# Seven half-size products in the down-projection of one token block, with weight differences made beforehand on VectorE

## The chip, the cores and the metric

The kernel runs on one core of one Trainium2 chip. The metric is device time in microseconds of one execution; the median of three runs of the kernel before is 2796.26 us (2793.03 to 2800.73). The engines are TensorE (PE; its weight loads are listed apart as PEld), VectorE (DVE), ScalarE (ACT), GpSimd (POOL) and SyncE (SP), which here issues nearly all DMAs.

## The reference

One layer of a network with two kinds of attention and a feed-forward part, on 2048 prompt tokens and 128 sample tokens (8 sequences of 16), all in fp32. What matters here is the feed-forward part behind it:

```python
def conv_ffn(h, buf, w_up, w_conv, b_conv, w_down):
    u = h @ w_up                                   # [S, 1024] @ [1024, 5632]
    ext = jnp.concatenate([buf.astype(u.dtype), u], axis=1)
    y = b_conv
    for j in range(CONV_W):                        # 3
        y = y + ext[:, j:j + S] * w_conv[j]
    gate, up = jnp.split(y, 2, axis=-1)
    out = (jax.nn.gelu(gate, approximate=True) * up) @ w_down   # [S, 2816] @ [2816, 1024]
    return out, ext[:, S:]
```

The layer then adds `rms_norm(ffn, norm_g[3])` to its input rows and returns them.

## The kernel before, in words

**Precision.** A matmul works on values in a shorter format (fp32r). So each fp32 operand is split into a high part (a cast by ScalarE) and a low part (the operand less the high part, by VectorE); `split`, in the profile L1265 (cast) and L1266 (subtraction). `mm3` (L93) makes three matmuls of each product: high x high (L95), high x low (L96), low x high (L97). A weight or activation piece is loaded as fp32 by DMA into a raw buffer, split, and used.

**Blocks.** The 17 token tiles of 128 rows are worked on in three blocks (FBLOCKS): tiles 0 to 5, 6 to 11, and 12 to 15 with the sample tile. For each block there is an up stage and a down stage.

**Up stage.** 22 column groups f of 128 gate and 128 up columns. The product is already made as seven products of half-size blocks in Winograd's form of Strassen's method (P1 to P7; `product`, L1411); the differences of the weights are made on VectorE in the first block (L1282) and kept in DRAM (`wsd`) for the others. Behind it come the convolution, GELU and the product of gate and up, giving a row buffer `gt` (128 columns x 768 tokens), which is stored to DRAM as `gd` (L1519). While the last groups run, the first tiles of `gd` are fetched back (`fetch`, L1454) and split (`split_g`, L1465).

**Down stage.** For each half `dh` of the 1024 output columns: six accumulators in PSUM, one per token tile, 512 columns each; for each of the 22 k (128 rows of w_down) 6 tiles x 3 matmuls of 128 x 512, the tile of g being the stationary and the weights the moving operand. `load_down` (L1311) loads and splits the weights in chunks of four k, one chunk ahead, into buffers `wh` and `wl` (two each). Tiles of g go through `w3` buffers, four of them, so two pairs of high and low. At the end of a half `evacuate` (L1334) copies the accumulators (VectorE, L1340) and sums the squares (ScalarE, L1344); the halves go to DRAM (f0d, f1d). In the same stage `ahead.step()` is called once per k: it advances `h2_units` (L1057 and on: loading, scaling and transposing the rows of the next block, and making its seven activation operands B) and `later` (L1369): scaling the finished rows of the block before (VectorE, L1376), adding the input (GpSimd, L1377) and storing (GpSimd, L1378).

**Buffers.** Raw pieces of 512 columns come from `quad` (tag "q", 11 buffers), rows of 1024 from `row` (tag "yq", 4 buffers). Loads wait for a free buffer.

**Order.** The program is written in the order of the loops; a planner built into the framework then reorders each engine's instructions by an estimated timeline. Each engine, and SP's queue of DMA issues, runs in order: an instruction that waits holds back all behind it. `tc.keep_in_program_order` fixes the order of some DMAs against each other.

## Time and profile before

| | |
|---|---|
| median of three runs | 2796.26 us (2793.03 to 2800.73) |
| the profiled execution's span, first to last instruction | 2784.7 us |
| busy: PE / DVE / ACT / POOL | 2723.8 / 1876.3 / 1409.1 / 437.4 us |
| up stages of the three blocks, roughly | 1313 to 1641, 1836 to 2154, 2349 to 2616 us |
| down stages, roughly | 1641 to 1836, 2155 to 2349, 2618 to 2777 us |

The profile is of one execution, and its times are microseconds from its first instruction. Nothing is listed of that execution's own time around the span; the median of the runs is 11.6 us above it. A row of groups reads: line, engine, operation, output <- inputs (buffer numbers left out), shapes, count | busy time, mean duration of one in ns | idle time of the engine just before them, and what ended it. Durations of successive operations on one engine overlap a little, so busy time is less than count times mean. A row of windows gives the stretch, its length, then busy us (and instructions) of each engine, the granted TensorE clock, the DMA share and GB/s.

### The profile page before, as it was taken

The numbers are of one execution on the slowest core, as the hardware profiler recorded it, in microseconds if no ns is written. First come the engines' busy times: TensorE is split into PE (matmuls) and PEld (weight loads), VectorE is DVE, ScalarE is ACT, GpSimd is POOL, SyncE is SP. The second block draws the span as 40 slices with busy tenths as digits, with TensorE's granted clock in tenths as the row PEclk, the third lists the DMA queues.
The fourth block names the chain that finished last, engine by engine and source line by source line (L and its number), as shares of the span: only waits on it lengthen the run. The fifth ranks groups of instructions, "written<-read, shape, count | busy, mean of one in ns | idle before, by whom it ended". The sixth has DMA issues, their size and how long they took to land.

```text
span 2784.7 us, 47088 instructions
## 1 busy us (share of the span) xinstructions
PE 2723.8 (98%) x16587; PEld 2548.3 (92%) x16587; DVE 1876.3 (67%) x3447; ACT 1409.1 (51%) x2836; POOL 437.4 (16%) x895
## 2 busy tenths in 40 slices
PE   8999999999999999999999999999999999999998
PEld 7899999998899998888999988899999878999887
DVE  5344455656556668666999986457877864888855
ACT  4355555644356666544454555345455543555543
POOL 1000010212000003244111110011111310222220
PEclk9999999999999999999999999999999999999999
DMA  5544355557555555356655455644544774555585
GB/s 185 155 119 136 103 174 162 164 157 217 162 173 148 144 179 171 107 176 227 187 172 167 167 176 174 219 142 153 160 152 141 276 263 152 172 179 180 192 309 190
DMA packets 311883, 486.05 MB, mean 175 GB/s; under 512 B 55426, under 2 KB 150622, under 8 KB 311518
## 3 DMA queue, kind: packets, MB, share of 16 engines
q1 hardware_dynamic: 271134, 442.92, 50.1%
q10 hardware_dynamic: 38592, 33.83, 3.6%
q0 software_dynamic: 1920, 6.29, 0.6%
q8 instruction: 130, 2.13, 0.3%
q14 instruction: 107, 0.88, 0.1%
HBM read 359.36 MB, written 126.70 MB: 175 GB/s over the span
## 4 chain that ended last, share of the span: by engine, by line
PE 55%; DVE 2%; DMA 1%; issue 1%; ACT 1%; POOL 1%; SPq 0%; DVEq 0%; POOLq 0%; ACTq 0%
PE uec L95 6%; PE uec L96 6%; PE uec L97 6%; PE dn L97 4%; PE dn L96 4%; PE dn L95 4%; PE ua L97 3%; PE ua L95 3%; PE ua L96 3%; PE dnm L97 2%; PE dnm L95 2%; PE dnm L96 2%; PE wo L97 2%; PE wo L95 2%; PE wo L96 2%; PE ub L96 1%
## 5 line engine op out<-in xcount | busy, mean ns | idle before, releaser
L95 PE MATMUL uec<-B,wuh 128*128 128x384 f32 (+1 forms) x720 | 234.9, 328 | 2.2 <-DVE uu L1419 1.1
L96 PE MATMUL uec<-B,wuh 128*128 128x384 f32 (+1 forms) x720 | 235.1, 327 | 0.0
L97 PE MATMUL uec<-B,wul 128*128 128x384 f32 (+1 forms) x720 | 233.9, 327 | 0.0
L1266 DVE TENSOR_TENSOR gl<-gr,gh 128x768 fp32r<-128x768 f32 (+3 forms) x141 | 120.4, 863 | 145.8 <-ACT gh L1265 144.5
L1265 ACT CAST gh<-gr 128x768 fp32r<-128x768 f32 (+3 forms) x141 | 102.0, 735 | 200.1 <-PE dn L96 183.2
L1265 ACT CAST wuh<-wu 128x512 fp32r<-128x512 f32 x255 | 141.7, 617 | 112.1 <-PE uec L96 103.2
L95 PE MATMUL dn<-wdh,gh 128*128 128x512 f32 x466 | 182.4, 391 | 2.3 <-DVE ug L1419 2.3
L96 PE MATMUL dn<-wdl,gh 128*128 128x512 f32 x466 | 183.4, 394 | 0.0
L97 PE MATMUL dn<-wdh,gl 128*128 128x512 f32 x466 | 167.9, 396 | 0.0
L1266 DVE TENSOR_TENSOR wul<-wu,wuh 128x512 fp32r<-128x512 f32 x255 | 164.6, 683 | 2.8 <-DMA x2d<-mx 2.8
L393 DVE CUSTOM_DVE_ANT_0 tmp<-s,nb 128x640 f32<-128x640 f32 (+4 forms) x128 | 94.4, 737 | 96.6 <-PE s L383 94.8
L95 PE MATMUL vo<-wi_h,hT 128*128 128x256 f32 x544 | 155.1, 285 | 0.6 <-DVE mt L199 0.6
L97 PE MATMUL vo<-wi_h,hT 128*128 128x256 f32 x544 | 155.6, 286 | 0.0
L96 PE MATMUL vo<-wi_l,hT 128*128 128x256 f32 x544 | 154.8, 285 | 0.0
L95 PEld LDWEIGHTS uec<-B,wuh 128*128 128x128 f32 x720 | 135.0, 188 | 4.2 <-DVE uu L1419 1.6
L95 PE MATMUL qk<-hT,wi_h 128*128 128x384 f32 (+1 forms) x384 | 128.7, 335 | 7.4 <-ACT qk_st L224 6.6
L96 PEld LDWEIGHTS uec<-B,wuh 128*128 128x128 f32 x720 | 135.2, 188 | 0.2
L97 PEld LDWEIGHTS uec<-B,wul 128*128 128x128 f32 x720 | 135.1, 188 | 0.0
L406 DVE TENSOR_TENSOR ptl<-pt,pth 128x640 fp32r<-128x640 f32 (+4 forms) x128 | 93.6, 737 | 57.1 <-ACT pth L405 56.0
L394 ACT ACTIVATE tmp<-tmp,mn 128x640 f32<-128x640 f32 (+4 forms) x128 | 97.6, 762 | 64.6 <-DVE mn L393 61.9
L96 PE MATMUL qb<-hT,wi_h 128*128 128x384 f32 (+1 forms) x384 | 127.8, 333 | 0.0
L96 PE MATMUL qk<-hT,wi_h 128*128 128x384 f32 (+1 forms) x384 | 127.6, 332 | 0.0
(412 smaller groups left out, 8873.0 us busy)
## 6 DMA issues: line engine op xcount, KB each, us to landing
wu<-in_w_up SPq DMA_DIRECT2D x220, 256.0 KB, 4.1
wu<-wsd SPq DMA_DIRECT2D x176, 256.0 KB, 4.2
wdr<-in_w_down SPq DMA_DIRECT2D x132, 256.0 KB, 5.6
gr<-gd SPq DMA_DIRECT2D x78, 384.0 KB, 3.6
wi_raw<-in_w_in SPq DMA_DIRECT2D x52, 512.0 KB, 4.0
wsd<-ws SPq DMA_DIRECT2D x88, 256.0 KB, 2.8
gd<-g SPq DMA_DIRECT2D x44, 384.0 KB, 3.5
kraw<-kTd SPq DMA_DIRECT2D x112, 128.0 KB, 3.2
```

The source lines that it names most:

```text
L95: nc.tensor.matmul(out, ah, bh, start=start, stop=False, skip_group_check=onto)
L96: nc.tensor.matmul(out, ah, bl, start=False, stop=False, skip_group_check=onto)
L97: nc.tensor.matmul(out, al, bh, start=False, stop=stop, skip_group_check=onto)
L393: nc.vector.tensor_tensor_reduce(o_, s_, b_, 1.0, 3e38, ALU.add, ALU.min, accum_out=mn)
L394: nc.scalar.activation(tmp[:, :n], tmp[:, :n], AF.Exp, bias=mn, scale=-1.0, accum_out=rsum[:, i % 4, hh:hh + 1])
L406: nc.vector.tensor_tensor(s.ptl[:, sl, qc], ptv, s.pth[:, sl, qc], op=ALU.subtract)
L1265: nc.scalar.copy(h, r)
L1266: nc.vector.tensor_tensor(l, r, h, op=ALU.subtract)
```

## The change: what it does

In the second block (FAST = (1,)) the down-projection is computed with the same scheme of seven products. G is cut into A11, A12, A21, A22 (token tiles 0 to 2 or 3 to 5; the first or the last 11 of the 22 k), w_down into B11, B12, B22, B21 in the same way (11 k each, 512 columns each). The weight operands T1 to T4 are differences of the four B blocks.

- `folds` loads w_down in 22 pieces of [128, 4, 256] into `row` buffers, makes four differences on VectorE and stores them in DRAM (`wtd`). One half of a piece's work is done in two of three k of the first block's down stage, and in three of four column groups of the second block's up stage.
- The second block's up stage runs through the columns in the order 0, 11, 1, 12, ... . `store_a` stores A11, A12, A22 and the four sums and differences S1 to S4, which are made in place in the `gt` buffers of the two columns (four VectorE operations of 384 columns); the buffer of column f is held until that of f + 11 is there. A21 alone isn't needed.
- The second block's down stage is a sequence of seven products of 11 k x 3 tiles. Three of the six accumulators make a set; products 0, 2, 4 and 6 add up in set 0, products 1, 3 and 5 are in set 1. `leave` takes a set out while the other is used (ScalarE copies after products 0, 2, 4, 6; VectorE additions after 1, 3, 5). `ahead.step()` is called once every two k.
- Weights are loaded in chunks of four k as before (`down_rows`); a chunk now serves 36 matmuls, not 72. A tile of A holds two k of 384 tokens (`fetch_a`, `split_a`).
- w_down is laid out in DRAM in the four blocks; the other blocks' loads have the same sizes.
- `quad` has 12 buffers, `row` 6, `drs` 2; the scratch memory for GpSimd's DMAs is 4096 bytes.

```diff
+NK = NF // 2
+FAST = (1,)
+ORDERS = [[f for k in range(NK) for f in (k, k + NK)] if b in FAST else list(range(NF)) for b in range(3)]
...
-        return ffn.p3.tile([P, 512], F32, tag="q", name=name, bufs=11)
+        return ffn.p3.tile([P, 512], F32, tag="q", name=name, bufs=12)
...
-        return ffn.p3.tile([P, D], F32, tag="yq", name=name, bufs=4)
+        return ffn.p3.tile([P, D], F32, tag="yq", name=name, bufs=6)
...
+    def folds():
+        v4 = lambda t: t.rearrange("p (a n) -> p a n", a=4)
+        def load(k, c):
+            t = v4(row(f"fold{k}_{c}"))
+            tc.keep_in_program_order(nc.sync.dma_start(t, v4(I["w_down"][k])[:, :, c * 256:(c + 1) * 256]))
+            return t
+        def combine(t):
+            a, b, c, d = [t[:, i] for i in range(4)]
+            for o, x, y in ((a, b, a), (b, c, b), (c, c, a), (d, d, c)):
+                nc.vector.tensor_tensor(o, x, y, op=ALU.subtract)
+        for k in range(NK):
+            for c in range(2):
+                t = load(k, c)
+                yield
+                combine(t)
+                tc.keep_in_program_order(nc.sync.dma_start(v4(wtd[k])[:, :, c * 256:(c + 1) * 256], t))
+                yield
...
+    SEQUENCE = [("A11", B11, 0, False), ("A12", B21, 1, False), ("S2", T2, 0, True), ("S4", B22, 1, False),
+                ("S3", T3, 0, True), ("S1", T1, 1, False), ("A22", T4, 0, True)]
...
+        def store_a(f, gt):
+            put = lambda what, k, src: nc.sync.dma_start(ad[b, what][:, k, :], src)
+            first, second = gt[:, 0:384], gt[:, 384:768]
+            if f < NK:
+                put("A11", f, first)
+                held[f] = gt
+                return
+            k = f - NK
+            put("A12", k, first)
+            put("A22", k, second)
+            gt1 = held.pop(k)
+            a11, a21, a12, a22 = gt1[:, 0:384], gt1[:, 384:768], first, second
+            nc.vector.tensor_tensor(a11, a11, a21, op=ALU.subtract)
+            nc.vector.tensor_tensor(a21, a21, a22, op=ALU.add)
+            nc.vector.tensor_tensor(a22, a22, a11, op=ALU.subtract)
+            nc.vector.tensor_tensor(a12, a12, a22, op=ALU.subtract)
+            for what, src in (("S3", a11), ("S1", a21), ("S2", a22), ("S4", a12)):
+                put(what, k, src)
...
-        for f in range(NF):
+        for fi, f in enumerate(ORDERS[b]):
...
-            nc.sync.dma_start(gd[b][f][:, :nt * P], gt[:, :nt * P])
+            if fast:
+                store_a(f, gt)
+                if fi % 4 < 3:
+                    next(fold, None)
+            else:
+                nc.sync.dma_start(gd[b][f][:, :nt * P], gt[:, :nt * P])
...
+            for p, (_, _, set_, onto) in enumerate(SEQUENCE):
+                for c in range(3):
+                    wh, wl = pend
+                    if c < 2:
+                        pend = load_product(b, p, c + 1)
+                    elif p < 6:
+                        pend = load_product(b, p + 1, 0)
...
+                    for k in range(4 * c, min(4 * c + 4, NK)):
+                        i = 6 * p + k // 2
+                        if k % 2 == 0:
+                            if i >= 1:
+                                split_a(i + 1)
+                                fetch_a(i + 4)
+                        wk = slice(k % 4 * 512, k % 4 * 512 + 512)
+                        ah, al = parts[i]
+                        for j in range(3):
+                            tt = slice(k % 2 * 384 + j * P, k % 2 * 384 + (j + 1) * P)
+                            mm3(sets[set_][j], ah[:, tt], al[:, tt], wh[:, wk], wl[:, wk],
+                                start=not onto and k == 0, stop=k == NK - 1, onto=onto)
+                        steps += 1
+                        if steps % 2 == 0:
+                            ahead.step()
+                leave(p)
...
+                    if b == 0 and (dh * NF + k) % 3 < 2:
+                        next(fold, None)
...
-    nc = bacc.Bacc("TRN2", target_bir_lowering=False, num_devices=1)
+    nc = bacc.Bacc("TRN2", target_bir_lowering=False, num_devices=1, dynamic_dma_scratch_size=4096)
```

154 lines of the change are left out of this document (127 added, 27 removed).

## The prediction

> **What bounds the kernel now.** I read the page's engine lines, its slices and its chain first, then the busy time by stage.
>
> ```profile
> span 2784.7 us, 47088 instructions
> ...
> PE 2723.8 (98%) x16587; PEld 2548.3 (92%) x16587; DVE 1876.3 (67%) x3447; ACT 1409.1 (51%) x2836; POOL 437.4 (16%) x895
> ...
> PE   8999999999999999999999999999999999999998
> ...
> PEclk9999999999999999999999999999999999999999
> ...
> PE 55%; DVE 2%; DMA 1%; issue 1%; ACT 1%; POOL 1%; SPq 0%; DVEq 0%; POOLq 0%; ACTq 0%
> ```
>
> TensorE is busy in every slice, at a granted clock of nine tenths or more, and it holds the chain: a matmul that goes is time that goes, as long as the engines that feed TensorE keep up. By stage (up of the first block, its down, up of the second, its down; columns: length, then busy time of PE, PEld, DVE, ACT, POOL, clock, DMA share, GB/s):
>
> ```profile
> 1313.00:1641.00 328.00, 322.00 (x1827) 318.55 (x1825) 302.79 (x457) 167.79 (x266) 61.74 (x87) 0.99 0.54 179
> 1655.00:1836.00 181.00, 180.42 (x805) 146.72 (x804) 101.61 (x140) 87.11 (x146) 5.02 (x17) 1.00 0.56 184
> 1840.00:2150.00 310.00, 310.00 (x1781) 310.00 (x1780) 239.98 (x357) 156.93 (x257) 41.49 (x92) 1.00 0.48 154
> 2166.00:2349.00 183.00, 182.60 (x812) 147.55 (x811) 115.07 (x151) 85.37 (x145) 35.07 (x41) 1.00 0.68 232
> ```
>
> The stage that the change rewrites is the last row: 183 us, TensorE without a gap, VectorE at 63%.
>
> **The change, part by part.**
>
> *Matmuls.* The second block's down stage has 22 k x 6 tiles x 2 halves x 3 = 792 matmuls of 512 columns; seven products of 11 k x 3 tiles x 3 make 693. The timeline of that stage gives the distance from one to the next:
>
> ```profile
> 2311.10 0.39 PE L95 MATMUL dn<-wdh,gh 128*128 128x512 f32 x1
> ...
> 2315.94 0.39 PE L95 MATMUL dnm<-wdh,gh 128*128 128x512 f32 x1
> ```
>
> Between these two starts lie 21 steps, 4.84 us, so 0.2305 us each. 99 x 0.2305 = 22.8 us go. The accumulators lie in two sets, and each is emptied while the other is filled for 99 x 0.2305 = 22.8 us, so I cost their emptying, and the step into the next block, at nothing; without that cover three copies of 0.68 us would stand on the path once a product.
>
> *VectorE and the feed of the seven products.* In steady state a tile of A (two k, 384 columns each) serves 18 matmuls as a tile of g did, so the splitting of A costs what that of g cost. But each weight piece now serves 9 matmuls, not 18: 77 pieces are split, not 44, and a chunk of four lasts 36 x 0.2305 = 8.3 us, not 16.6. The stage is not even: the preparation of the third block (h2_units) and the finished rows of the first (later) fill its first half, and they still take one step per 18 matmuls, so they fall on the first four products. The windows of before, its VectorE groups in 2166-2258, two of 2258-2349, one of GpSimd, and the DMA sum of 2166-2258:
>
> ```profile
> 2166.00:2258.00 92.00, 91.60 (x417) 73.35 (x416) 76.57 (x100) 51.07 (x88) 32.85 (x33) 1.00 0.79 273
> ...
> 2258.00:2304.00 46.00, 46.00 (x201) 37.43 (x201) 20.53 (x28) 19.73 (x36) 2.22 (x8) 1.00 0.77 267
> 2304.00:2349.00 45.00, 45.00 (x197) 36.77 (x196) 17.98 (x24) 14.56 (x23) 0.00 (x0) 1.00 0.38 114
> ```
>
> ```profile
> L1266 DVE TENSOR_TENSOR gl<-gr,gh 128x768 fp32r<-128x768 f32 x18 | 21.3, 1184 | 3.5 <-ACT gh L1265 3.4
> L1266 DVE TENSOR_TENSOR wdl<-wdr,wdh 128x512 fp32r<-128x512 f32 x22 | 16.4, 804 | 0.0
> L1376 DVE SCALAR_TENSOR_TENSOR f<-f,drs,norm_row 128x512 f32<-128x512 f32 x12 | 10.0, 831 | 4.5 <-DMA f<-f0d 4.5
> L1085 DVE SCALAR_TENSOR_TENSOR x2r<-x2r,n_rs,g 128x1024 f32<-128x1024 f32 x4 | 6.2, 1540 | 5.2 <-POOL n_rs L84 5.2
> ...
> L1340 DVE COPY fr<-dnm 128x512 f32<-128x512 f32 x2 | 1.3, 678 | 0.0
> ...
> L1106 DVE TENSOR_TENSOR B<-b,B 128x256 fp32r<-128x256 f32 x3 | 1.2, 412 | 0.0
> ```
>
> ```profile
> L1266 DVE TENSOR_TENSOR gl<-gr,gh 128x768 fp32r<-128x768 f32 x21 | 20.1, 958 | 47.1 <-ACT gh L1265 47.1
> L1266 DVE TENSOR_TENSOR wdl<-wdr,wdh 128x512 fp32r<-128x512 f32 x18 | 11.5, 685 | 3.8 <-ACT wdh L1265 3.8
> ```
>
> ```profile
> L1377 POOL TENSOR_TENSOR f<-f,x 128x512 f32<-128x512 f32 x12 | 22.0, 1834 | 35.7 <-DVE f L1376 26.2 <-DMA gr<-gd 9.5
> ```
>
> ```profile
> DMA packets 10786, 25.08 MB, mean 273 GB/s; under 512 B 1280, under 2 KB 1280, under 8 KB 10779
> ```
>
> VectorE worked 76.6 of 92 us. To that come 22 more weight subtractions (another 16.4 us), the accumulator additions in place of copies (6 x 0.68 - 1.3 = 2.8 us), and the last five differences of A that run over from the up stage (5 x 0.55 = 2.8 us): 98.6 us. TensorE needs for four products 396 x 0.2305 = 91.3 us and some 3 us of transposes, 94 us. So VectorE asks for 4 us more than there are, and its in-order waits come on top: 3.4 + 4.5 + 5.2 = 13.1 us in the rows above, of which a part vanishes when VectorE itself is late. The loss is between 0 (the pieces of the fifth product may come one chunk, 8.3 us, late, and the last products have room) and 98.6 + 13.1 - 94 = 18 us. I take 8, nearer to the busy sum than to the waits, since those rows show waits of an engine that had time. The last three products: 33 x 0.685 + 18 x 0.96 + 6 x 0.68 = 44 us of VectorE in 68: covered. ScalarE in the first four: 51.1 + 22 x 0.62 + six copies and three squares of some 0.6 = 70 of 94 us: covered. DMA: 25.1 MB + 22 x 0.26 MB + ten late stores of 0.2 MB = 33 MB in 94 us, 350 GB/s, against these (the first from the third block's down stage):
>
> ```profile
> 2650.00:2680.00 30.00, 30.00 (x131) 24.31 (x130) 18.82 (x25) 11.08 (x17) 13.98 (x15) 1.00 1.05 400
> 2189.00:2212.00 23.00, 23.00 (x109) 18.76 (x109) 20.70 (x26) 13.83 (x23) 10.20 (x11) 1.00 0.97 345
> ```
>
> 400 GB/s went by while TensorE ran without a gap, so it fits, but with nothing to spare; that keeps 18 us in the range.
>
> *Up stage of the second block.* Its order of columns (f, f + 11) costs nothing: the loads are the same. VectorE gets 44 operations of 384 columns and 28 of 256 (7 of the 22 weight pieces, four differences each):
>
> ```profile
> L1493 DVE TENSOR_TENSOR x<-x,uec 128x384 f32<-128x384 f32 x22 | 12.2, 553 | 11.3 <-PE uec L97 11.2
> ```
>
> 240.0 + 44 x 0.55 + 28 x 0.41 = 276 of 310 us, 89%. Two of the four differences overwrite a tile whose store must have landed, and block VectorE until then; the stores of the sums stand in SP's queue ahead of the next weight loads and wait for them. The page's rows for such a store and for a weight load:
>
> ```profile
> gd<-g SPq DMA_DIRECT2D x44, 384.0 KB, 3.5
> ...
> wdr<-in_w_down SPq DMA_DIRECT2D x132, 256.0 KB, 5.6
> ```
>
> The built order puts four other VectorE operations, some 2.7 us, between the product and the first overwrite, so about 1 us is left per pair, 11 us, and VectorE is occupied for 287 of 310 us, 93%. The first block's up stage stands at 302.8 of 328 us, 92%, and what it pays is seen in TensorE's waits of 1313-1641:
>
> ```profile
> PE ua L97 <- DVE wul L1266: 3.0, 2, 1.6
> PE uec L95 <- DVE uu L1419: 1.1, 1, 1.1
> PE uec L95 <- DVE ug L1419: 1.0, 1, 1.0
> ```
>
> Between 0 and 5; much of the 5 stands at that stage's beginning, so I take 2. 77 stores of 0.2 MB for 22 of 0.39 and 7 pieces of 1 MB moved add 14 MB, 45 GB/s to 154: hidden.
>
> *Down stage of the first block.* 15 of the 22 pieces: 60 differences x 0.41 = 24.7 us on VectorE, 126 of 181 us; 15 loads and 15 stores of 512 KB make 184 into 270 GB/s. Each store waits in SP's queue for VectorE, and behind it the weight loads. Covered by VectorE's 30% and by buffers; without that a store holds the queue some 2 us, 30 in all. Between 0 and 3, I take 1.
>
> *Buffers and the small DMA scratch.* 12 and 6 buffers for 11 and 4 change the planner's order from the first up stage on: between -4 and +4, taken 0 (that stage's waits above are about all there is to gain). GpSimd's 12 stores in the seven products are one per 7.8 us; a smaller ring could make one wait for the one before, 0 to 3 us, taken 0, since GpSimd is busy 33 of 92 us.
>
> Sum: -22.8 + 8 + 2 + 1 = -11.8 us. The profiled span of 2784.7 us becomes 2772.9. The median of the runs shown, 2796.26, is 11.6 above that span; I leave that as it is and get **2784.4 us**.
>
> **The rivals.** *All hidden.* If the first four products keep TensorE fed and the others cost 1, it is -21.8: 2774. For it: VectorE had 15 us idle in 92; against: it needs all of them.
>
> *GpSimd and VectorE exclude each other.* While GpSimd adds (22.0 us), the subtraction of g took 1184 ns against 958, that of weights 804 against 685: 18 x 0.226 + 22 x 0.119 = 6.7 us lost. With VectorE full there is no idle time in which the rest could hide: 22.0 - 6.7 = 15.3 us more, net +3.5, 2800. The Trainium skill, SBUF — State Buffer, section "Who interferes with whom", says that a VectorE instruction with two SBUF inputs and a GpSimd instruction that reads SBUF lock each other out for a whole instruction; by that rule this rival holds, and the rows above agree that there is a price but show under a third of it.
>
> *Slower: weights late.* Of twelve small buffers the preparation of the third block uses eight, so in the first products loads may not run ahead. Then a chunk's last piece comes after its landing, four casts and a subtraction:
>
> ```profile
> wdr<-in_w_down SPq DMA_DIRECT2D x18, 256.0 KB, 5.7
> ...
> x2r<-x2d SPq DMA_DIRECT2D x4, 512.0 KB, 7.2
> ```
>
> 5.7 + 4 x 0.62 + 0.69 = 8.9 us, against 8.3 for a chunk of four and 6.2 for one of three: 14 x 0.6 + 7 x 2.7 = 27 us late over the stage, which with the 3 us of the other stages gives +7 (2804); each further us of landing adds 21. From 5.8 us on it is slower beyond noise; at 6.5 it is 2821. For it: DMA near its highest rate and the row of 7.2. Against it: ScalarE hardly waited for weights before (4.7 us in the stage).
>
> ```profile
> ACT wdh L1265 <- DMA wdr<-in_w_down: 4.7, 5, 1.3
> ```
>
> *It saves nothing,* because the steps between matmuls lengthen by a seventh: +3, 2799. Nothing speaks for it; the shapes are the same.
>
> **How the numbers follow.** 0.3% of 2796 is 8.4 us, about what a measurement of this kernel can tell from no change. Forecast 0.42 (its own range 2776 to 2792; 0.34 below 2787.9, 0.08 above), all hidden 0.20, exclusion 0.12, weights late 0.22, no saving 0.04. Faster 0.54, same 0.08 + 0.12 + 0.04 = 0.24, slower 0.22. The range goes from 2771 (nothing lost, and the buffers gain 3) to 2806, where it leaves out most of the slower case and little else.
>
> **What would show it.** 99 fewer matmuls, the seven products ending some 14 us sooner after their start than 183 us; gaps of TensorE in the first four, ended by VectorE's subtractions, none in the last three; VectorE over 95% in the first four; 0 to 5 us of gaps in the second up stage. The prediction is wrong if those gaps exceed 20 us, if a DMA ends them, or if the unchanged stages move by more than 4 us.

## The result: slower by 0.4%, and the profile after

The changed kernel takes 2807.65 us (median of five runs, 2801.63 to 2811.27) against 2794.01 us for the kernel before on the same chip: 1.0040 times as long, 95% interval 1.0029 to 1.0051. That is outside the predicted range and on the other side of the kernel before. The profiled execution of the changed kernel is the fastest of its five, 6.0 us below the median, so the stages below account for that execution and not for the median. Its page begins with the span and the busy time by engine:

```profile
span 2799.9 us, 47375 instructions
...
PE 2717.2 (97%) x16488; PEld 2541.4 (91%) x16488; DVE 1940.9 (69%) x3610; ACT 1426.7 (51%) x2879; POOL 458.8 (16%) x895
```

The 99 matmuls are gone (16587 to 16488), yet the span grew, and TensorE's busy time fell by 6.6 us, not by 22.8. Slices of 70 us don't show why. So I cut each trace by what TensorE works on: an up stage runs from the first to the last start of its up matmuls, and the rest of the block, its down stage with the turn into the next, follows. The times are starts of matmuls in the trace, in us:

| kernel | ahead of the blocks | up 1 | down 1 | up 2 | down 2 | up 3 | down 3 | span |
|---|---|---|---|---|---|---|---|---|
| before, as profiled first | 1313.5 | 338.0 | 185.0 | 328.3 | 184.5 | 276.1 | 159.5 | 2784.7 |
| before, profiled again | 1316.0 | 335.4 | 185.1 | 328.3 | 185.3 | 276.1 | 164.9 | 2791.1 |
| **after** | 1318.4 | **341.9** | **197.7** | 331.3 | **170.5** | 277.9 | 162.2 | 2799.9 |

Three stages moved by much. The seven products (down 2) save 14.0 us. The first block's down stage, where the weight differences are made, loses 12.7. The first up stage, in which the change alters no instruction but has other buffer counts, loses 4 to 6.5. The rows of the windows for down 1, up 2 and down 2, first of the kernel after, then of the kernel before (columns as in the prediction):

```profile
1660.30:1858.00 197.70, 187.06 (x818) 150.48 (x817) 124.78 (x202) 91.18 (x151) 9.73 (x20) 0.98 0.75 247
1858.00:2189.30 331.30, 329.96 (x1879) 327.24 (x1878) 281.28 (x447) 168.54 (x280) 45.71 (x101) 1.00 0.62 195
2189.30:2359.80 170.50, 163.92 (x708) 131.43 (x707) 132.68 (x189) 103.86 (x188) 39.01 (x47) 0.97 0.81 282
```

```profile
1651.50:1836.50 185.00, 183.77 (x819) 149.31 (x818) 104.02 (x143) 90.67 (x152) 5.94 (x20) 1.00 0.55 180
1836.50:2164.80 328.30, 327.77 (x1873) 326.21 (x1872) 255.19 (x377) 167.95 (x278) 44.55 (x101) 1.00 0.48 156
2164.80:2349.30 184.50, 183.89 (x820) 148.51 (x819) 116.35 (x153) 86.82 (x148) 35.43 (x41) 1.00 0.68 230
```

In down 1 the matmuls are the same, but TensorE is idle for 10.6 us instead of 1.2, and its mean clock is 0.98. VectorE is at 63%, DMA at 75%: neither is full. So the shares don't tell the cause; the waits do. (A row of waits reads: who waited <- what ended the wait: us in total, number of waits, the longest.) TensorE's waits in that stage of the kernel before:

```profile
PE dn L95 <- DVE ug L1419: 0.6, 1, 0.6
PE dnm L95 <- ACT wdh L1265: 0.5, 1, 0.5
PE dnm L95 <- ACT gh L1265: 0.3, 1, 0.3
```

In the kernel after, first TensorE's waits, then the longest of VectorE, then those of SP's queue that have to do with the pieces (L1168 issues the load of a piece, L1174 makes its differences, L1181 issues its store, L1505 fetches a tile of g):

```profile
PE dnm L100 <- DVE fr L1380: 4.8, 1, 4.8
PE dnm L102 <- DVE gl L1296: 3.0, 3, 1.4
PE dnm L100 <- ACT gh L1295: 1.1, 2, 0.8
PE h2T_pt L1101 <- DVE x2r L1093: 1.1, 1, 1.1
```

```profile
DVE fold L1174 <- DMA fold<-in_w_down: 38.1, 11, 7.1
```

```profile
SPq L1505 <- DMA wtd<-fold: 16.1, 8, 3.9
SPq L1168 <- DMA wtd<-fold: 12.5, 5, 3.9
SPq L1505 <- DVE fold L1174: 11.4, 4, 5.4
```

VectorE stands 38 us in front of differences whose piece hasn't landed. It works in order, so everything behind them stands too. SP's queue waits for pieces' stores to land before it may issue a fetch of g or the next piece, because both take their buffers from `row`. The largest gap, 4.75 us, lies at the turn between the two halves of the stage. The timeline there:

```profile
1755.57 0.60 SPq L1168 DMA_DIRECT2D fold<-in_w_down  x1
...
1760.90 0.43 DVE L1174 TENSOR_TENSOR fold<-fold 128x256 f32<-128x256 f32 x1 [5.89 <-DMA fold<-in_w_down]
1761.24 0.68 DVE L1380 COPY fr<-dnm 128x512 f32<-128x512 f32 x1
...
1762.08 0.76 PE L100 MATMUL dnm<-wdh,gh 128*128 128x512 f32 x1 [4.75 <-DVE fr L1380]
```

The load was issued at 1755.57; VectorE waits 5.89 us for it with nothing else done, and behind that difference stands the copy of the first accumulator (`fr`), without which the second half can't start. The wait list names "DVE fr" as the releaser; the cause is one instruction further back, and it is a DMA.

The gap then costs more than its length. In the last four rows below the clock column drops to a half for two stretches of 3.41 us, and in the first of them TensorE starts again only at 1762.08. The first two rows are from another place of the same kernel; the clock is the third number from the end:

```profile
80.43:83.84 3.41, 0.88 (x5) 0.80 (x5) 1.33 (x5) 1.00 (x2) 0.00 (x0) 0.99 0.11 25
83.84:87.25 3.41, 3.41 (x13) 3.41 (x12) 1.72 (x5) 1.52 (x3) 0.00 (x0) 0.51 0.33 100
1756.25:1759.66 3.41, 1.07 (x5) 0.54 (x3) 0.00 (x0) 0.00 (x0) 0.00 (x0) 1.00 0.94 281
1759.66:1763.08 3.42, 1.00 (x3) 0.84 (x4) 2.18 (x5) 0.85 (x3) 0.19 (x1) 0.51 0.35 137
1763.08:1766.49 3.41, 3.41 (x10) 2.64 (x9) 3.41 (x7) 2.67 (x7) 0.19 (x2) 0.50 0.84 246
1766.49:1769.90 3.41, 3.41 (x16) 2.83 (x15) 0.99 (x2) 1.97 (x5) 1.11 (x5) 0.99 0.92 282
```

Between 1763.08 and 1766.49 TensorE is busy throughout and has 10 matmuls where the next stretch has 16. It is busy for 1.00 + 3.41 us of the 6.8 at half clock, so these cost up to 2.2 us. So of down 1's 12.7 us, 4.8 are the gap, up to 2.2 the half clock behind it, and 4.9 small waits for `gl`, `gh`, `x2r` and others (6.3 us against 1.4 before); I can't place the remaining 0.8.

### The profile page after: what moved, and what is told of

It reads as the page before. It is cut to its first block, busy times and chain, and to the rows that moved or that the text cites. A ratio compares the mean times of both kernels' runs of the same rounds, so it can differ in the third digit from the quotient of the medians.

```text
span 2799.9 us, 47375 instructions
## 1 busy us (share of the span) xinstructions
PE 2717.2 (97%) x16488; PEld 2541.4 (91%) x16488; DVE 1940.9 (69%) x3610; ACT 1426.7 (51%) x2879; POOL 458.8 (16%) x895
## 5 line engine op out<-in xcount | busy, mean ns | idle before, releaser
L102 PE MATMUL qk<-hT,wi_l 128*128 128x384 f32 (+1 forms) x384 | 128.0, 333 | 0.0
L101 PE MATMUL qb<-hT,wi_h 128*128 128x384 f32 (+1 forms) x384 | 128.0, 333 | 0.0
L1295 ACT CAST gh<-gr 128x768 fp32r<-128x768 f32 (+3 forms) x92 | 65.0, 719 | 122.8 <-PE dn L101 105.5
L102 PE MATMUL qb<-hT,wi_l 128*128 128x384 f32 (+1 forms) x384 | 127.3, 332 | 0.0
L100 PE MATMUL qb<-hT,wi_h 128*128 128x384 f32 (+1 forms) x384 | 127.2, 331 | 0.0
L1296 DVE TENSOR_TENSOR wdl<-wdr,wdh 128x512 fp32r<-128x512 f32 x165 | 108.9, 702 | 22.3 <-ACT wdh L1295 22.0
```

Source lines behind the costliest of these rows:

```text
L100: nc.tensor.matmul(out, ah, bh, start=start, stop=False, skip_group_check=onto)
L101: nc.tensor.matmul(out, ah, bl, start=False, stop=False, skip_group_check=onto)
L102: nc.tensor.matmul(out, al, bh, start=False, stop=stop, skip_group_check=onto)
L1295: nc.scalar.copy(h, r)
L1296: nc.vector.tensor_tensor(l, r, h, op=ALU.subtract)
```

## The experiments

Times are given with the ratio to the kernel before, measured on the same chip, and its 95% interval; stages are read from each run's profile as above. Theory A was at first that the differences hold back VectorE; rivals were the buffers, the DMA bandwidth, and the place in DRAM. The first four expectations count the turn into the next stage with the first down stage and give 195 us before and 208 after for it; in the tables, as in the later expectations, these are 185.0 and 197.7.

### Which part costs

The kernel after with the old down-projection and no pieces (only buffers, DRAM layout and scratch changed), the same with the pieces made but unused, and the kernel after without pieces:

```diff
 # buffers_alone
-FAST = (1,)
+FAST = ()
-    fold = folds()
+    fold = iter([])
 # folds_alone
-FAST = (1,)
+FAST = ()
 # no_folds
-            src = I["w_down"][k] if blk < 4 else wtd[k]
+            src = I["w_down"][k]
-    fold = folds()
+    fold = iter([])
```

Expected of buffers_alone:

> No block is computed in seven products and no weight differences are made: what is left of the change is 12 and 6 buffers for 11 and 4, the two buffers of drs, the smaller scratch and the layout of w_down. Theory A (the 15 us that the changed kernel lost outside the second block are VectorE waiting in the first block's down stage for pieces to land, and the rest is chance of the execution): as before within 4 us, first down stage about 195 us. Theory B (the buffers' other order costs the 4.9 us ahead of the feed-forward part, the 3.9 us in the first up stage and the 2.6 us in the third down stage): 8 to 12 us slower than before, in those stages.

Expected of folds_alone:

> The second block is computed as before; 15 of the 22 weight pieces are loaded, differenced and stored in the first block's down stage and never used. Theory A: 10 to 14 us slower than the kernel with the buffers alone, all of it in the first down stage (208 against 195 us), with waits of VectorE for the pieces' loads of 30 to 40 us there. Theory B: less than 4 us slower than the kernel with the buffers alone.

Expected of no_folds:

> Left out: the weight differences; the seven products read blocks of w_down in their place. Theory A: the second block's up and down stage together 10 to 14 us shorter than before, the first down stage as before, so 10 to 14 us faster than before in all (2780 to 2785) plus or minus 4 for the execution. Theory B: the same less 8 to 12 us, so no faster than 2790.

| kernel | us | ratio | up 1 | down 1 | up 2 | down 2 |
|---|---|---|---|---|---|---|
| buffers_alone | 2802.28 | 1.0029 (1.0018 to 1.0040) | 339.9 | 185.1 | 328.3 | 184.9 |
| folds_alone | 2814.09 | 1.0074 (1.0059 to 1.0089) | 339.9 | 197.9 | 328.3 | 183.7 |
| no_folds | 2793.64 | 0.9998 (0.9987 to 1.0009) | 340.7 | 186.6 | 332.9 | 168.8 |

The pieces cost 2814.09 - 2802.28 = 11.8 us, as theory A expected, and all of it stands in down 1: 197.9 against 185.1. Of buffers_alone and no_folds, theory B's forecasts came true (8.1 us more than before; no faster than 2790), though the stage that clearly shows it is up 1 alone. Even without pieces the seven products don't gain over the kernel before, though their stage saves 15.7 us: the buffers' part takes 8 us of it and the second up stage 4.6.

### The buffers' part

The kernel before with only the small DMA scratch; the kernel before once more; with eleven unused tensors in DRAM; with only the buffer counts:

```diff
 # scratch_alone
-    nc = bacc.Bacc("TRN2", target_bir_lowering=False, num_devices=1)
+    nc = bacc.Bacc("TRN2", target_bir_lowering=False, num_devices=1, dynamic_dma_scratch_size=4096)
 # dram_shift
+    unused = [dt_([P, 2048], f"unused{k}") for k in range(11)]
 # bufs_only: the scratch of scratch_alone, and
-        ... tag="q", name=name, bufs=11)
+        ... tag="q", name=name, bufs=12)
-        ... tag="yq", name=name, bufs=4)
+        ... tag="yq", name=name, bufs=6)
-        ... name=f"drs{tiles[j]}", bufs=1)
+        ... name=f"drs{tiles[j]}", bufs=2)
```

> The kernel before with the smaller scratch for GpSimd's DMAs and nothing else; each engine's order is the same as before. The buffers, scratch and layout together were 8.1 us slower than before, and 6.4 us of that stood in the profile ahead of the feed-forward part, whose order was the same. If the scratch (or the addresses that it moves) costs that: 5 to 9 us slower than before. If it was the buffers' new order behind that part, and the rest chance of one profile: as before within 3 us.

> The kernel before, profiled once more. If the part ahead of the feed-forward part differs by chance between executions, it takes 1317 to 1323 us here and not 1313; if it is always 1313 to 1315, the 5 to 11 us more in the other profiles are of the change.

> The kernel before with 11 unused tensors of 1 MB ahead of others in DRAM, so that those behind lie elsewhere; each engine's order is the same as before. If the places in DRAM cost the 3 to 8 us that all changed kernels took longer ahead of the feed-forward part: 3 to 8 us slower than before, in that part. If not: as before within 2 us.

> The kernel before with 12 and 6 buffers, two buffers of drs and the small scratch, no other layout in DRAM; each engine's order is that of the kernel with buffers, scratch and layout, which took 8.1 us more than before. If the buffers' order costs it: 5 to 9 us slower than before, the first up stage near 340 us against 335 to 338. If the other places in DRAM cost it: as before within 3 us.

| kernel | us | ratio | ahead of the blocks | up 1 |
|---|---|---|---|---|
| before_again | 2794.62 | 1.0008 (0.9998 to 1.0019) | 1316.0 | 335.4 |
| scratch_alone | 2793.22 | 1.0004 (0.9995 to 1.0013) | 1316.8 | 336.4 |
| dram_shift | 2791.88 | 1.0007 (0.9995 to 1.0019) | 1321.8 | 336.6 |
| bufs_only | 2793.30 | 1.0016 (1.0007 to 1.0024) | 1318.9 | 340.2 |

Scratch and DRAM addresses do nothing that can be told from no change. `dram_shift` has 1321.8 us ahead of the blocks, as the theory of the places wanted, but 6.0 us of that are half clock (last section; the two profiles of the kernel before have 1.7 and 3.3), and the time as a whole didn't follow. The 1316.0 of `before_again` lie between the bounds of its expectation. The layout of w_down was not run by itself: `buffers_alone` has it and `bufs_only` doesn't, and their intervals overlap. The counts alone cost 4.5 us (0.07 to 0.24%), and where it shows is up 1. TensorE's waits there, of the kernel after; the prediction has those of the kernel before (3.0, 1.1, 1.0):

```profile
PE ua L102 <- DVE wul L1296: 3.9, 2, 3.0
PE uec L100 <- DVE uu L1608: 2.7, 4, 1.0
PE uec L100 <- DVE x L1587: 2.5, 2, 1.3
```

The planner orders the first columns otherwise when more buffers are free: each engine's order is the same in the two profiles of the kernel before and in `scratch_alone`, and another in `bufs_only`. Two later kernels, which are the version `late_spread` below with one count taken back, tell which count:

```diff
 # late_spread_q11
-        ... tag="q", name=name, bufs=12)
+        ... tag="q", name=name, bufs=11)
 # late_spread_r5
-        ... tag="yq", name=name, bufs=6)
+        ... tag="yq", name=name, bufs=5)
```

> The version before this one with 11 quarter buffers in place of 12, as in the kernel before. If the twelfth quarter buffer is what orders the transfers of the first up stage otherwise (340 us there against 335 to 338 us), that stage comes back to 336 to 338 us and the time is 2 to 4 us below the version before this one; if the row buffers do it, no difference.

> The version with late pieces and other steps with 5 row buffers in place of 6 (12 quarter buffers). If the row buffers order the transfers of the first up stage otherwise, that stage comes back to 336 to 338 us and the time is 2 to 4 us lower than with 6; if the quarter buffers do it, no difference, or a loss of 1 to 3 us where the pieces have one buffer less.

With 11 quarter buffers up 1 is 336.0 us, with 5 row buffers 340.2 (342.4 in `late_spread`). `folds_own_rows` below, with twelve quarter and four row buffers, has 339.9. So it is the twelfth quarter buffer that goes with the order that costs there, by one profile of each. But the times, 2794.14 and 2793.44 us (0.9993, 0.9982 to 1.0004, and 0.9995, 0.9986 to 1.0004), can't be told from `late_spread`'s 2793.49: the 2 to 4 us that I expected in the median didn't come.

### Why the pieces cost 12 us in down 1

Four kernels change how the pieces are made, one where. `early_load` issues the load of a piece three turns ahead of its differences. `pool_fold` makes the differences on GpSimd; `pool_all` also issues the pieces' loads and stores from GpSimd. `folds_own_rows` is folds_alone with buffers of their own for the pieces and four row buffers. `late_fold` makes no pieces in the first half of down 1, but one half piece per k in its second half and one per column of up 2 instead:

```diff
 # early_load
+        todo = [(k, c) for k in range(NK) for c in range(2)]
+        t = load(*todo[0])
+        yield
+        for i, (k, c) in enumerate(todo):
+            ahead_ = load(*todo[i + 1]) if i + 1 < len(todo) else None
+            yield
+            combine(t)
+            ...
 # pool_fold (pool_all: also nc.sync to nc.gpsimd in the load and the store)
-                nc.vector.tensor_tensor(o, x, y, op=ALU.subtract)
+                nc.gpsimd.tensor_tensor(o, x, y, op=ALU.subtract)
 # folds_own_rows (from folds_alone)
-            t = v4(row(f"fold{k}_{c}"))
+            t = v4(ffn.p3.tile([P, D], F32, tag="fd", name=f"fold{k}_{c}", bufs=2))
-        ... tag="yq", name=name, bufs=6)
+        ... tag="yq", name=name, bufs=4)
 # late_fold
-                if fi % 4 < 3:
-                    next(fold, None)
+                next(fold, None)
-                    if b == 0 and (dh * NF + k) % 3 < 2:
+                    if b == 0 and dh == 1:
```

> Each weight piece's load is issued three turns ahead of its differences, not one (some 15 us, not 6). Theory A: VectorE's waits for the pieces fall from 38 to under 10 us, the first down stage from 208 to about 197 us, in all 8 to 12 us faster than the changed kernel (2796 to 2800). Rival (not the wait but the DMA traffic of 31 MB, or SP's queue behind the pieces' stores, takes the time): the first down stage stays above 204 us and the whole at 2804 or more.

> The weight differences are made on GpSimd instead of VectorE; loads, stores and their bytes are the same. Theory A (VectorE standing in order before a piece that has not landed is the cost): the first down stage returns from 198 to 188 us or less, the whole to about 2797 us. Rival (DMA traffic and SP's queue are the cost): the first down stage stays at 195 us or more, the whole at 2805 or more.

> The weight pieces are loaded, differenced and stored by GpSimd alone, its own DMA queue included; the bytes are the same, but SP's queue and VectorE have nothing to do with them. If the first down stage pays for waits that stand in order ahead of other work (VectorE's for a piece, SP's for a finished piece or a free row): it returns from 197 to 190 us or less, the whole to 2798 or less. If it pays for the bytes (245 GB/s in place of 181): it stays at 194 us or more.

> The pieces are made as in the version with pieces alone (nothing reads them, the down-projection is the old one), but they live in two buffers of their own, and the row buffers are back to four, which g's tiles and the output rows have for themselves. Theory that shared row buffers cause the loss of the first block's down stage (a piece that waits for VectorE holds a buffer, the next load waits in the queue for it, and g's tiles stand behind that): the stage, 197.9 us with pieces in the row buffers and 184 to 186 us in kernels without pieces, falls to 190 us or less. Theory that the first half of the stage is crowded as such (conversion of weights, copies of the accumulators and pieces all on VectorE at the turn of the halves, the piece's load ahead of all of them in the queue): it stays at 195 us or more.

> 11 of the 22 pieces are made in the second half of the first down stage, where VectorE works 40% of the time, and 11 in the second up stage; none in the first half. If the cost belongs to the crowded first half: the first down stage falls from 198 to about 190 us, the second up stage pays 1 to 3 us more, the whole is 3 to 7 us faster than the changed kernel. If each piece costs the same wherever it stands (0.8 us): the first down stage falls to 194 us and the second up stage gains as much, no change in all.

| kernel | us | ratio | down 1 | up 2 | down 2 |
|---|---|---|---|---|---|
| early_load | 2801.94 | 1.0022 (1.0010 to 1.0034) | 193.6 | 330.4 | 169.7 |
| pool_fold | 2805.77 | 1.0044 (1.0028 to 1.0060) | 196.7 | 332.8 | 168.5 |
| pool_all | 2801.55 | 1.0044 (1.0029 to 1.0060) | 192.1 | 344.9 | 168.3 |
| folds_own_rows | 2807.92 | 1.0046 (1.0033 to 1.0059) | 190.3 | 328.2 | 186.0 |
| late_fold | 2789.10 | 0.9997 (0.9988 to 1.0007) | 186.0 | 328.2 | 172.5 |

`early_load` fell between its two forecasts. VectorE's waits for pieces went from 38.1 to 24.4 us in 8 waits, not to under 10, and down 1 by 4.1 us; so it took away only a part of the waits that it was to remove. (The 31 MB of its expectation are 30 transfers of 512 KB, 15.7 MB.)

`pool_fold` came out as the rival of theory A said. VectorE no longer waits for pieces, and down 1 is still 196.7 us: now the store of a piece stands in SP's queue until GpSimd has made the differences, 31 us in all, and TensorE's big gap is ended by the high part of a tile of g. TensorE's row, the queue's, and one of VectorE's in down 1:

```profile
PE dnm L100 <- ACT gh L1295: 8.1, 2, 7.3
```

```profile
SPq L1181 <- POOL fold L1174: 31.1, 10, 5.1
```

```profile
L1296 DVE TENSOR_TENSOR wdl<-wdr,wdh 128x512 fp32r<-128x512 f32 x40 | 32.3, 860 | 11.0 <-ACT wdh L1295 11.0
```

But this run doesn't only take away VectorE's waits. A difference takes 0.73 to 1.79 us on GpSimd where it took some 0.42 on VectorE, and VectorE's own subtractions get longer beside it: 860 ns for weights against 685 in down 1 of the kernel after, 1073 against 954 for g. So it shows that moving the differences doesn't help; that VectorE's waits cost nothing it doesn't show.

`pool_all` takes the pieces out of SP's queue altogether; then fetches of g wait for the buffers that the pieces hold, 46.6 us in nine waits (the first row, of the queue in down 1), and TensorE waits for weights in up 2 (the rows behind it). Its 192.1 us in down 1 lie between the bounds of its expectation, its time above the 2798 of the first forecast:

```profile
SPq L1505 <- DMA wtd<-fold: 46.6, 9, 7.5
```

```profile
PE ua L100 <- ACT wuh L1295: 6.7, 4, 2.3
PE ua L102 <- DVE wul L1296: 2.9, 1, 2.9
```

`folds_own_rows`, with the differences left where they are in VectorE's order, brings down 1 from 197.9 to 190.3 us. It fell neither in the one theory's bound (190 or less) nor in the other's (195 or more), but it is nearer to the first: 7.6 of the 12.8 us go when pieces and g tiles no longer wait for each other's buffers. VectorE's waits for pieces, 36.7 us in folds_alone, fall to 20.4 with that, so the two links aren't separated by it. TensorE's waits for the copy and for `gl`, 4.9 and 3.2 us in folds_alone, are now

```profile
PE dnm L100 <- DVE fr L1380: 1.2, 1, 1.2
...
PE dnm L102 <- DVE gl L1296: 0.3, 1, 0.3
```

`late_fold` leaves the shared buffers, the in-order queues and the total of the bytes as they are, and moves the pieces out of the first half, where the preparation of the second block (transposes, their differences and splits) also runs. There are 11 pieces in down 1 for 15, but closer together, all in its second half. Its halves of down 1 (windows):

```profile
1643.30:1740.00 96.70, 94.74 (x439) 77.64 (x439) 68.63 (x98) 57.39 (x97) 6.29 (x15) 1.00 0.58 189
1740.00:1839.30 99.30, 98.88 (x428) 79.85 (x427) 58.54 (x99) 37.15 (x63) 1.81 (x7) 1.00 0.85 286
```

286 GB/s in the second half, more than the 247 of the kernel after, and TensorE is idle for 0.4 us, though VectorE waits 13.8 us for pieces there. So bandwidth isn't the cause, and a wait of VectorE for a piece costs TensorE only where the work behind it is due. The cause that the runs leave is a chain of in-order waits over three places: a piece's load waits in the queue for a row buffer, VectorE (or the store) waits for the piece, g's tiles wait for both, in the half of the stage that has the most other work. Loosening the chain at one place or another gave 4 to 12 us of the stage back, but for making the differences on GpSimd (1 us). The chain itself is read from the waits; how much each link costs by itself in the kernel after stays open, since no run changed one link and left the others' waits as they were.

### What is left in the seven products

`spread` is the kernel after with the preparation of the third block taken in steps 2 and 4 of five instead of every second one. `late_spread` has this and late_fold's edit. `late_ends` is late_spread with two turns of the pieces in even columns of up 2, so that they are finished before the seven products begin; `late_ends_h2` begins the preparation ten steps later as well:

```diff
 # spread, late_spread
-                        if steps % 2 == 0:
+                        if steps % 5 in (2, 4):
 # late_ends
                 next(fold, None)
+                if fi % 2 == 0:
+                    next(fold, None)
 # late_ends_h2
-                        if steps % 5 in (2, 4):
+                        if steps > 10 and steps % 2 == 0:
```

> The preparation of the third block and the finished rows of the first advance in two of five k of the seven products instead of one of two, so that they reach over five and a half products instead of four. If VectorE's load in the first four products costs the 8 to 9 us that the second down stage lost against 22.8 us: 2 to 5 us faster than the changed kernel, and gaps of TensorE there fall from 6 us to under 3. If the gaps come of single waits of the transposes for VectorE, not of its load: no difference beyond 2 us.

> Pieces made in the second half of the first block's down stage and in every column of the next up stage, and the last block's intermediate made ahead in other steps of the seven products. Theory that the placement of the pieces was the loss: the first block's down stage 186 us, the second block's up stage 328 us as in the version with late pieces alone, its down stage 167 to 172 us; the time 4 to 7 us below the kernel before (0.9975 to 0.9985 of it). Theory that late pieces and the other steps get in each other's way: no faster than the version with late pieces alone, 0.9997.

> The version with late pieces and other steps, and in the second block's up stage an even column takes two turns of the pieces instead of one, so that the last piece is done by the fifteenth column of 22. Theory that pieces left over in the queue of VectorE at the turn into the seven products (four of their differences stand at 2184 to 2194 us of that version, ahead of the splits that the first product waits for) cost TensorE's first gaps there (9 us in all): these shrink to 4 us or less, the stage falls from 170.8 to 166 us, the time to 0.9975 of the kernel before. Theory that it is the preparation of the third block alone: no difference from 0.9994.

> The version before this one, with the preparation of the third block begun ten steps later in the seven products (and then in every second step). Theory that this preparation costs TensorE's first gaps: they go, the stage falls to 164 to 167 us, the time to 0.997 of the kernel before. Theory that it only moves them: the gaps stand later in the stage, and the time is within 0.001 of the version before this one.

| kernel | us | ratio | down 1 | up 2 | down 2 | up 2 + down 2 |
|---|---|---|---|---|---|---|
| before | | | 185.0 | 328.3 | 184.5 | 512.8 |
| after | 2807.65 | 1.0040 (1.0029 to 1.0051) | 197.7 | 331.3 | 170.5 | 501.8 |
| spread | 2799.21 | 1.0018 (1.0008 to 1.0029) | 197.0 | 332.2 | 167.6 | 499.8 |
| late_spread | 2793.49 | 0.9994 (0.9985 to 1.0003) | 186.1 | 328.2 | 170.8 | 499.0 |
| late_ends | 2791.47 | 0.9985 (0.9974 to 0.9996) | 186.4 | 337.1 | 164.6 | 501.7 |
| late_ends_h2 | 2791.36 | 0.9993 (0.9983 to 1.0002) | 186.7 | 335.9 | 162.5 | 498.4 |

`spread` takes 2.9 us off down 2, and its ratio, 1.0018, lies at the edge of that of the kernel after. In `late_spread` down 1, up 2 and down 2 came out as the first theory forecast, but the time didn't (0.9975 to 0.9985 was expected). Beside the kernel before, profiled again, down 2 saves 14.5 us; up 1 takes 7.0 of them, the part ahead of the blocks 8.3, of which 3.5 are half clock. Up 3 takes 2.3; it has 277.5 to 279.4 us in every kernel with the seven products against 276.1 in all others, a loss of the next block's stage that I haven't traced. TensorE's waits at the beginning of the seven products were

```profile
PE dn L100 <- ACT wdh L1295: 4.1, 1, 4.1
PE h2T_pt L1101 <- DVE x2r L1093: 2.8, 1, 2.8
PE dn L100 <- ACT ah L1295: 1.5, 1, 1.5
```

With the pieces finished early (`late_ends`) two groups of small waits are left, 3.5 us, and down 2 is 164.6 us: the expected fall, so those waits came from pieces left over. With the preparation begun later as well (`late_ends_h2`) it is 162.5, 22 us less than before: there the 99 matmuls that went save nearly their whole 22.8 us in the stage. The time didn't follow (0.997 was expected). And in `late_ends` up 2 grows from 328.2 to 337.1 us. VectorE works 287 of 337 us there and is late, by TensorE's waits in that stage:

```profile
PE uec L100 <- DVE uu L1608: 2.1, 2, 1.8
PE ua L102 <- DVE wul L1296: 1.5, 2, 0.8
```

Behind the wait of 1.8 us stands a half-clock stretch of 3.4 us. TensorE's idle time of 4.5 us and half of that stretch make some 6 of the 8.9 us; the rest I can't place. The two stages together stay at 498 to 502 us whatever the order. Of all kernels only `late_ends` is faster than the kernel before by its interval, by 0.04 to 0.26%, which is less than the 0.3% that I took as the least to be told; `late_ends_h2` has the same median and an interval that holds 1. I don't call either a gain.

## Why the prediction was wrong, by its own steps

- *Matmuls, -22.8:* right. 99 are gone, and in the last three products the stream runs without a gap at nearly the old step of 0.2305 us. In the timeline 28 steps lie between these two starts, 0.2325 us each:

```profile
2319.70 0.39 PE L100 MATMUL dnm<-wdh,ah 128*128 128x512 f32 x1
...
2326.21 0.39 PE L100 MATMUL dn<-wdh,ah 128*128 128x512 f32 x1
```

- *VectorE and the feed of the seven products, +8:* right in size, and the size is luck. Down 2 fell by 14.0 us, -22.8 + 8 = -14.8 was forecast. The picture was right in that the waits lie in the first four products and none in the last three. But VectorE isn't short of time: it works 85.7 of 96 us there, 89%, where 98.6 of 94 were added up. The longest wait is one of the third block's transposes for a single VectorE instruction, and the waits come to 6.5 us against next to none before; what else is lost may be the half clock behind them (TensorE works 9.7 us at it, up to 4.9 lost), which no step had. First four products, last products (windows), then TensorE's waits of the stage:

```profile
2190.00:2286.00 96.00, 89.42 (x386) 70.74 (x385) 85.68 (x122) 62.95 (x117) 29.57 (x35) 0.95 0.89 310
2290.00:2352.00 62.00, 62.00 (x269) 50.47 (x268) 38.92 (x57) 34.64 (x61) 7.85 (x11) 1.00 0.78 270
```

```profile
PE h2T_pt L1101 <- DVE t L1127: 2.9, 1, 2.9
PE dn L101 <- DVE wdl L1296: 1.3, 2, 1.0
```

- *Up stage of the second block, +2:* right in size, 331.3 against 328.3, +3.0, with 1.3 us of waits. That VectorE's added work is the reason is not shown: with more pieces there (late_fold) the stage takes 328.2 us, with none (no_folds) 332.9.
- ***Down stage of the first block*, "Covered by VectorE's 30% and by buffers ... Between 0 and 3, I take 1":** this is the step that failed. It measured +12.7 in the profile and 11.8 by folds_alone less buffers_alone. I had named the price of the lost cover, 30 us of held queue, and then trusted shares: VectorE idle for 30% and six buffers. Idle time doesn't cover an engine that works in order and is given an instruction whose input was ordered 6 us earlier: its idle time becomes the wait. And the added buffers were no cover, since pieces hold them: with buffers of their own down 1 loses 5.2 us and not 12.8 (folds_own_rows against buffers_alone). late_fold shows it from the other side: eleven pieces packed into the second half cost about 1 us (186.0).
- *Buffers and scratch, "taken 0", -4 to +4:* off. buffers_alone is +0.18 to +0.40%, 5 to 11 us; bufs_only 2 to 7 us. Only the scratch and the places in DRAM were 0. This is the second wrong term; the counts made a new order with longer waits, and I had given a loss no more weight than a gain.
- Together: -11.0 us in the second block against -12.8 forecast, +12.7 in down 1 against +1, and some 5 in up 1 against 0. That the base was one execution, below the median by about 10 us, did not matter: the ratio is against runs on the same chip.
- *The rivals.* "Weights late" gave 2804 to 2821, and 2807.65 lies there, but it is not what happened: waits for the seven products' weights are 1.3 and 0.6 us in down 2. Exclusion of GpSimd and VectorE was no loss of the change, but it is there, and the means by which I priced it hide it. Of the 16 VectorE instructions in the first four products that overlap an addition of GpSimd, nine take 0.5 to 1.1 us longer than the median of their like beside no GpSimd work, and the others as long; that is 7.9 us in all, an estimate from the trace, where the rival had 22.0. The kernel before has 10.4 us of the same in 2166-2258, so it was in the base already and grew no larger. A subtraction of weights took 734 ns in the mean against 685 in the last three products. The mean's row, then a pair with its like behind it (first the addition, 1.29 us, then a VectorE instruction of 2.33 us that starts just behind it, and the next of its kind, 1.27):

```profile
L1296 DVE TENSOR_TENSOR wdl<-wdr,wdh 128x512 fp32r<-128x512 f32 x40 | 28.3, 734 | 1.5 <-ACT wdh L1295 1.3
```

```profile
2224.78 1.29 POOL L1417 TENSOR_TENSOR f<-f,x 128x512 f32<-128x512 f32 x1
2224.83 2.33 DVE L1093 SCALAR_TENSOR_TENSOR x2r<-x2r,n_rs,g 128x1024 f32<-128x1024 f32 x1 [0.46 <-POOL n_rs L89]
...
2228.61 1.27 DVE L1093 SCALAR_TENSOR_TENSOR x2r<-x2r,n_rs,g 128x1024 f32<-128x1024 f32 x1
```

"It saves nothing" fell with down 2, "all hidden" with the 8.8 us that down 2 lacks of 22.8. My own sign that the prediction is wrong, stages that the change leaves alone moving by more than 4 us, came true (up 1, by 3.9 us against the first profile of the kernel before and 6.5 against the second), and it was the right one to look at first.

## What to carry to other kernels

Before side work is put beside a stage, look at the queues it enters, not at the shares: an operation put on an in-order engine a few us after its load is issued stops that engine, and a buffer tag shared with the stage's own tiles lets the side work stop the stage's loads; a place away from the turn of accumulators, and buffers of its own, are worth more than idle per cent. A saved matmul is worth its time only in a stage that is fed, so cost the stage that pays for the preparation with the same care as the one that is shortened. And count a gap of TensorE of more than about 2 us at its length and up to 1.7 us more for each stretch of 3.41 us at half clock behind it.

## What the hardware showed that I had not expected

The granted clock falls to a half in stretches of 3.41 us or twice that (the last of each profile, behind the last matmul, has other lengths), and these begin on a fixed grid: within one execution all starts agree modulo 3.413 us to within 0.004 us, and the phase differs from execution to execution. I cut the 20 traces of this case (one of each kernel) on that grid, left out the beginning and the end of each, and took windows that ran at full clock themselves. How often the next one ran at half clock, by how long TensorE was idle in the window (by the profile's ends of matmuls, which are modelled):

| idle in the window, us | windows | followed by half clock |
|---|---|---|
| under 1.4 | 15820 | 2 |
| 1.4 to 1.8 | 95 | 16 |
| 1.8 to 2.0 | 37 | 30 |
| over 2.0 | 75 | 75 |

So it is not the length of a gap that decides, but how it falls on the grid. The pair of rows at 80 us above shows a gap of 2.5 us inside one window, with half clock behind it. The kernel before has a gap of 3.2 us at the same place of its program, cut in two by the grid, and stays at full clock (0.51 above, 1.00 here):

```profile
77.78:81.19 3.41, 2.01 (x12) 1.59 (x11) 0.21 (x1) 0.00 (x0) 0.00 (x0) 1.00 0.06 10
81.19:84.60 3.41, 1.57 (x9) 1.57 (x10) 1.59 (x7) 1.68 (x4) 0.00 (x0) 1.00 0.17 52
84.60:88.02 3.42, 3.42 (x21) 3.16 (x20) 1.26 (x2) 0.83 (x2) 0.00 (x0) 1.00 0.44 112
```

The Trainium skill, TensorE: Matmul & The Clock Gate, section "Part 1: The HAM clock gate (the "warmup" mystery)", says that the clock is halved after an idle window of some 3.4 us and that these windows run freely, without regard to the kernel. The traces agree on the length and on the free phase; they differ on the condition, since a window that was idle for 2.0 of 3.41 us was enough each time.

Two things follow for this case. Part of the scatter between executions of one and the same instruction order is this: ahead of the blocks, where the change moves nothing, the time was 1312 to 1326 us over the 20 profiles, and the half clock there took up to 1.7 to 9.9 us of it (half of what TensorE worked in the stretches). Counted off, 1308 to 1321 us are left, so most of that spread stays unexplained. And from the first up stage on, these stretches cost up to 11.8 us in the profile after, against 1.4 and 3.1 in the two of the kernel before: counted off, the kernel after would need 1469.7 us there against 1469.9 and 1472.0. That is an account of one execution each, not a run in which they were taken away, which I could not make; but it suggests that much of what the change lost stands behind its gaps, not in them.
